# Eight query blocks moved into four Strassen pairs, with the scan beside the first output blocks and the attention beside the last

## The chip, the cores and the metric

The kernel runs on one core of one Trainium2 chip. The metric is the device time of one execution in microseconds, lower is better. TensorE (PE in the profile) multiplies matrices into PSUM; VectorE (DVE), ScalarE (ACT) and GpSimd (POOL) work on tiles in SBUF and PSUM; SyncE (SP) issues most of the DMA transfers. Each engine takes its instructions strictly in the order in which they were built.

## The reference

One layer of a hybrid decoder for 1024 prompt tokens and 8 sample tokens, which share the weights. All values are float32.

```python
def mixer_block(xn, ...):                      # xn = rmsnorm(x), width 1024
    sc_b, sc_c, sc_x, z, xbc, dt_raw, q, gates = split(xn @ w_in)
    y_a = (sc_b * conv3(sc_c * sc_x)) @ w_sc_out
    xs, bm, cm = split(silu(conv4(xbc) + bias))
    y_ssd = chunked_scan(xs, softplus(dt_raw + ...), -exp(a_log), bm, cm)   # 32 heads, 4 groups, chunks of 128
    y_b = group_rmsnorm((y_ssd + d * xs) * silu(z), groups=4) @ w_ssm_out   # 2048 -> 1024
    y_c = softmax(q @ k.T / 16) @ v  @ w_attn_o                             # 4 heads, 256 memory tokens
    g_a, g_b, g_c = split(sigmoid(gates))
    return (g_a * y_a + g_b * y_b + g_c * y_c) @ w_merge_o
x = x + mixer_block(rmsnorm(x)); x = x + swiglu(rmsnorm(x)); y = rmsnorm(x)
```

The sample tokens use their own recurrent states and their own cached keys and values (8 batches of 256 tokens).

## The kernel before

Activations lie transposed: 8 tiles of 128 features by 1032 tokens. A product in float32 precision is made of three matmuls, high times high, high times low and low times high, where a tile is split into a high part (ACT, lines 175 and 185) and a low part (DVE, lines 176 and 186).

**Two ways to make a block.** `gemm3` (lines 231 to 257) makes one block of 128 output features: 8 k-tiles, 3 thirds of 344 tokens, 3 matmuls each, so 72 matmuls of 344 columns (line 254). `strassen` (from line 379) makes two blocks at once with seven half-size products: 7 products, 4 k-tiles, 3 matmuls, two pieces of 256 and 260 tokens, so 168 matmuls (line 306). Its seven right-hand sides are called forms; one of them, T3, lies in the place of a quarter of the normalized input.

**Stages.** First the input is normalized. Then w_in is gone through in Strassen pairs: z, gates, the scan's inputs (X), the short convolution (C, B), with `gate_pair(22)` last. Then come 32 blocks of `gemm3` in a row: eight query blocks (`ps_q`, weights `wq0` to `wq7`), then three times eight output blocks, `wo00` to `wo07` (short convolution, from `sc_d`), `wo10` to `wo17` (first half of w_ssm_out, from `yb_d[0:8]`) and `wo20` to `wo27` (second half, from `yb_d[8:16]`). After them the attention output (`wo30` on, from `at_d`), the merge and the feed-forward part.

**What runs beside the 32 blocks.** A list `pend` holds small pieces, and each block takes `pace` of them at fixed places between its matmuls (`tick`). First `pend` holds the scan: four groups of eight chunks. A chunk brings small matmuls (`bp`, `xp`, `po`, `py`, `pss`), DVE and ACT work. After a group come `z_pieces` (times silu(z), sum of squares), then `group_norm`: matmuls `psny`, a root on ACT, the scaling of four tiles on DVE (line 1267) and their stores to `yb_d` (line 1270). Then `pend` holds the attention: scores `psa`, softmax, `psp`, values `psv`, and for the sample tokens keys and values read from the caches (`kc`, `vc`), scores on DVE (line 1676), `pso`, and at the end `s_back` (`psob`, line 1743), which writes the sample columns of `at_d`.

**Order.** The pieces give each instruction its place in the source order, and a scheduler with pools of buffers then sets the order on each engine. `out_in` and `out_ahead` load and split the eight inputs of a set of output blocks; the first block of a set (m = 0) goes through its k-tiles one at a time, so that it can begin when the first input is there.

Before the query blocks the T3 form must be turned back into the plain input: `again` reads four tiles again and `plain` splits them, inside `gate_pair(22)`.

Of the kernel before, what the change touches and what calls it, by code (L numbers as in the profile page):

```python
# [11 lines left out]
AF = mybir.ActivationFunctionType  # L12
# [5 lines left out]
P = 128  # L18
# [25 lines left out]
def tile_kernel(ctx: ExitStack, tc, a, o):  # L44
# [333 lines left out]

    def strassen(src1, src2, forms, nm, sums, outs, early=None, after_t3=None, ready=None, hook=None, add=False, begun=None, mid=None, t3_done=None):

# [90 lines left out]
    zs_d = dram("zs_d", [16, P, TT])  # L471
    r_d = dram("r_d", [1, TT])
    x2_d = dram("x2_d", [KD, P, TT])
# [30 lines left out]
    with tc.tile_pool(name="p0", bufs=1) as p0, tc.tile_pool(name="pop", bufs=1, space=PSUM) as pop:  # L504
# [214 lines left out]

        SY.dma_start(r_d, rbc[0:1, :])  # L720
    pmm[0] = mm_stack.enter_context(tc.tile_pool(name="pmm", bufs=2, space=PSUM))
# [182 lines left out]

    def q_step(i):
        def s():
            t = ev_tile(f"q{i}")
            gemm3(
                weights(wblock(w_in, C_Q + i * P), f"wq{i}"), xn, f"ps_q{i}",
                lambda n, c, ps: S.activation(t[:, c], ps, AF.Copy, scale=QS), *(() if i < 7 else ((0, 0, 0),)),  # L910
            )
            G.tensor_copy(qs[:, i, :], t[:, T:TT])
            S.dma_start(q_d[i], t[:, :TT])

        return [Step(wblock(w_in, C_Q + i * P), f"wq{i}", s)]

    def xbc_conv(ct, u, name):
# [31 lines left out]

    def plain_pair(col, dst, i, nm, func, hook=None, after_t3=None):  # L950

        os = []

        def outs():
            os.extend([pa_["u"](f"{nm}{i}"), pa_["u"](f"{nm}{i + 1}")])
            return os[0][:, HS[0]], os[0][:, HS[1]], None, os[1][:, HS[1]]

        pa = strassen(
            wblock(w_in, col + i * P), wblock(w_in, col + (i + 1) * P), xforms, f"{nm}{i}", pa_["s"], outs,
            hook=hook, after_t3=after_t3,  # L960
        )
        S.activation(os[0][:, :TT], os[0][:, :TT], func)
        S.dma_start(dst[i], os[0][:, :TT])
        S.activation(os[1][:, HS[1]], os[1][:, HS[1]], func)
        ins = S.activation(os[1][:, HS[0]], pa, func, scale=-1.0).ins
        S.dma_start(dst[i + 1], os[1][:, :TT])
        return ins
# [3 lines left out]

    def gate_pair(i, after_t3=None):
        return plain_pair(C_G, gt_d, i, "G", AF.Sigmoid, None, after_t3)

# [79 lines left out]
    def ssd_pieces(g, xg, bcg, hold):  # L1054
# [126 lines left out]

        out = [head] + ([None] * 4 if g == 0 else [])
        for c in range(NCK + 1):
# [146 lines left out]

    def again(rb):
        ts = []
        for kt in range(4):
            if kt % 2 == 0:
                ts.append(ev_tile(f"again{kt}"))
            b12 = ts[-1][:, HS[kt % 2]]
            SY.dma_start(b12, xT_d[kt][:, HS[1]])
            V.scalar_tensor_tensor(b12, b12, par("mix", kt), rb[:, HS[1]], op0=ALU.mult, op1=ALU.mult)
        return ts


    mem_stack = ExitStack()
# [135 lines left out]
    def load_group(g):  # L1478
        xg, bcg, _ = groups[g]
        for i, part in ((16, "ah"), (20, "al")):  # L1480
            t = act_tile(part, f"bc{i}{g}", F32)
            SY.dma_start(t, xs_d[i + g])
            bcg.append(t)
        for i in range(4):
            t = act_tile(("ah", "al")[i % 2], f"x{g}{i}", F32)

            for c in (slice(0, 2 * P), slice(2 * P, TT)) if g else (slice(0, TT),):
                SY.dma_start(t[:, c], xs_d[g * 4 + i][:, c])
            xg.append(t)

    def plain():
        loaded["wq0"] = load_raw(wblock(w_in, C_Q), "wq0")
        load_group(0)
        for kt in range(4):
# [10 lines left out]
    for name in ("ssr", "ssd", "ssy"):  # L1505
        pool[name] = ssd.enter_context(tc.tile_pool(name=name, bufs=2, side="right"))
    fillers = deque()
    for i in range(8):
        fillers.extend(q_step(i))

    acts = []

    ahead = deque()

    def out_load(src, k):
        t = ev_tile(f"in0{k}")
        SY.dma_start(t[:, :TT], src[k])
        ahead.append(t)

# [56 lines left out]

    split = []
    outs = deque()
# [16 lines left out]
    for g in range(GROUPS):  # L1595
# [888 lines left out]
```

## Time and profile before

| | |
|---|---|
| median of 3 runs | 2417.18 us (2413.96 to 2420.94) |
| the profiled execution | 2418.97 us, its span 2417.2 us |
| PE busy | 2388.3 us (99% of the span) |
| DVE busy, ACT busy | 1650.5 us (68%), 1101.1 us (46%) |
| DMA | 403.74 MB, mean 167 GB/s |
| first query block to first attention-output block (`wq0` to `wo30`) | 981.1 us to 1548.6 us of the span |

The table says that PE is nearly always busy; the profile's chain of work that ended last is 89% PE. A busy PE is not a PE at its peak, so the start times of neighbouring matmuls tell more than the busy share.

### The profile page before, as it was taken

What the parts mean: (1) busy time and instruction counts of PE and PEld (TensorE: products, weight loads), DVE (VectorE), ACT (ScalarE), POOL (GpSimd) and SP (SyncE); (2) the same over time, 40 slices, a digit from 0 to 9 for tenths busy, and PEclk for the clock granted to TensorE, in tenths of its full rate; (3) what the DMA queues carried; (4) which work ended last, traced back from release to release, by engine and by line L of the source; (5) the groups of instructions that cost most, each with busy time, mean ns of one, the idle gap of its engine ahead of it and who ended that gap; (6) DMA issues with size and microseconds to landing.
All of it is one profiled execution on the core that took longest, in us unless ns stands there. A gap on an engine that the chain in (4) does not pass through costs nothing.

```text
span 2417.2 us, 45099 instructions
## 1 busy us (share of the span) xinstructions
PE 2388.3 (99%) x18620; PEld 2305.3 (95%) x18620; DVE 1650.5 (68%) x2700; ACT 1101.1 (46%) x1794; POOL 129.3 (5%) x163
## 2 busy tenths in 40 slices
PE   8999999999999999999999999999999999999998
PEld 6999999999999999998998998899999999999998
DVE  6844677777777676568788664469687655567965
ACT  6643454555453543656656443214553333343423
POOL 0000000000000000223212000000000000000000
PEclk9999999999999999999999999999999999999999
DMA  6445423444354345768787787864346333354622
GB/s 201 140 149 166 132 88 115 134 147 128 109 158 119 101 140 167 234 214 279 257 286 238 234 321 242 276 215 145 118 159 175 103 96 105 93 182 151 194 90 78
DMA packets 348244, 403.74 MB, mean 167 GB/s; under 512 B 16014, under 2 KB 269054, under 8 KB 348031
## 3 DMA queue, kind: packets, MB, share of 16 engines
q1 hardware_dynamic: 324902, 337.60, 45.1%
q10 hardware_dynamic: 23137, 63.26, 6.8%
q8 instruction: 146, 2.39, 0.4%
q14 instruction: 59, 0.48, 0.1%
HBM read 284.65 MB, written 116.38 MB: 166 GB/s over the span
## 4 chain that ended last, share of the span: by engine, by line
PE 89%; DMA 4%; DVE 4%; ACT 1%; issue 1%; SPq 0%; ACTq 0%; DVEq 0%
PE po L254 8%; PE po L226 3%; PE ps_q L254 3%; PE pd L2295 1%; PE py L1130 1%; PE po L1121 1%; PE ps_z L226 1%; PE pss L1143 1%; PE G16m L306 1%; PE d00m L306 1%; PE G22m L306 1%; PE Z2m L306 1%; PE Z14m L306 1%; PE X4m L306 1%; PE Z12m L306 1%
## 5 line engine op out<-in xcount | busy, mean ns | idle before, releaser
L1073 ACT ACTIVATE r<-r,acum 128x128 f32<-128x128 f32 x256 | 79.3, 392 | 3.0 <-DMA r<-ac_d 2.4
L1106 POOL TENSOR_TENSOR xdd<-xdt,decst 128x512 f32<-128x512 f32 x32 | 51.1, 1596 | 248.3 <-DVE xdt L1102 246.1
L860 DVE SCALAR_TENSOR_TENSOR ax<-u,prm,ax 128x1024 f32<-128x1024 f32 x44 | 56.3, 1280 | 0.0
L1014 ACT ACTIVATE st<-st,es 128x128 f32<-128x128 f32 x128 | 41.4, 392 | 21.9 <-DMA st<-in_state_ssm_dram 19.1
L1564 DVE TENSOR_TENSOR yr<-po,yr 128x344 f32<-128x344 f32 x24 | 12.1, 514 | 45.9 <-PE po L254 32.5
L1100 DVE TENSOR_TENSOR r<-r,cbm 128x1024 f32<-128x1024 f32 x32 | 39.0, 1218 | 3.2 <-ACT r L1075 2.4
L1016 DVE SCALAR_TENSOR_TENSOR st<-sr,dts,st 128x128 f32<-128x128 f32 x128 | 40.3, 346 | 0.4
L1125 DVE TENSOR_TENSOR y<-po,ea 128x512 f32<-128x512 f32 x28 | 19.3, 689 | 25.4 <-PE po L1121 25.3
L1020 DVE SCALAR_TENSOR_TENSOR sr<-st,sr 128x128 f32<-128x128 f32 x128 | 35.3, 286 | 1.1
L1130 PE MATMUL py<-r,xdt 128*64 128x128 f32 x512 | 35.0, 279 | 0.7 <-DVE xdt L1102 0.7
L1676 DVE SCALAR_TENSOR_TENSOR kc<-kc,qb 128x256 f32<-128x256 f32 x64 | 24.2, 420 | 16.6 <-DMA qb<-qs_d 11.0
L1156 POOL TENSOR_TENSOR s<-s,cdec 128x512 f32<-128x512 f32 x28 | 34.8, 1244 | 4.1 <-DVE s L1149 3.5
L1143 PE MATMUL pss<-xdd,bT 128*128 128x512 f32 x64 | 33.0, 597 | 1.1 <-DVE y L1125 0.6
L1075 ACT ACTIVATE r<-r 128x1024 f32<-128x1024 f32 x32 | 33.8, 1056 | 0.6
L1130 PEld LDWEIGHTS py<-r,xdt 128*64 128x64 f32 x512 | 27.3, 136 | 5.0 <-DVE xdt L1102 1.4
L1121 PE MATMUL po<-bc,s 128*128 128x128 f32 x224 | 30.2, 278 | 0.8 <-DVE s L1149 0.8
L1121 PEld LDWEIGHTS po<-bc,s 128*128 128x128 f32 x224 | 28.0, 191 | 2.4 <-DVE s L1149 1.7
L1688 ACT ACTIVATE pr<-psa,mx 128x256 f32<-128x256 f32 x32 | 14.9, 473 | 29.7 <-DVE mx L1686 29.7
L863 DVE SCALAR_TENSOR_TENSOR ax<-u,prm,ax 128x1032 f32<-128x1032 f32 x22 | 28.3, 1287 | 0.0
L857 ACT ACTIVATE ax<-u,prm 128x1024 f32<-128x1024 f32 x22 | 27.4, 1246 | 1.2 <-ACT u L941 0.4
L1791 ACT CAST pTh<-psp 128x256 fp32r<-128x256 f32 x32 | 11.8, 374 | 32.9 <-DVE pTl L1792 24.0
L1102 DVE TENSOR_TENSOR xdt<-xp,dtT 128x512 f32<-128x512 f32 x32 | 22.0, 687 | 6.4 <-PE xp L1095 5.8
(8856 smaller groups left out, 9294.4 us busy)
## 6 DMA issues: line engine op xcount, KB each, us to landing
r<-ac_d SPq DMA_DIRECT2D x32, 512.0 KB
gt_d<-G ACTq DMA_DIRECT2D x24, 516.0 KB
gt<-gt_d SPq DMA_DIRECT2D x24, 516.0 KB
xs_d<-ax ACTq DMA_DIRECT2D x22, 516.0 KB
zs<-zs_d SPq DMA_DIRECT2D x16, 516.0 KB
yb_d<-x SPq DMA_DIRECT2D x16, 516.0 KB
in<-yb_d SPq DMA_DIRECT2D x16, 516.0 KB
st<-in_state_ssm_dram SPq DMA_DIRECT2D x32, 256.0 KB
```

What stands on the lines that cost most here:

```text
L226: PE.matmul(po, wt[:, ks], xc, start=(k == 0 and i == 0), stop=(k == nk - 1 and i == 2))
L254: PE.matmul(pss[t][:, :CW], wt[:, ks], x[:, c], start=(k == 0 and i == 0), stop=(k == nk - 1 and i == 2))
L306: last_mm[0] = PE.matmul(po, wt[:, ks], xc, start=(start and kt == 0 and i == 0), stop=(kt == 3 and i == 2), skip_group_check=True,).ins
L860: V.scalar_tensor_tensor(acc[:, :T], u[:, j : j + T], w[j], acc[:, :T], op0=ALU.mult, op1=ALU.add)
L1014: S.activation(st[:, i], st[:, i], AF.Copy, scale=es[:, g * 4 + i, b : b + 1])
L1016: V.scalar_tensor_tensor(st[:, i], rb, dts[:, g * 4 + i, b : b + 1], st[:, i], op0=ALU.mult, op1=ALU.add)
L1073: S.activation(r[:, j, :], r[:, j, :], AF.Relu, scale=-1.0, bias=acum[:, c, h : h + 1])
L1100: V.tensor_tensor(r, r, bc(cbm.unsqueeze(1), [P, HPG, P]), op=ALU.mult)
L1106: G.tensor_tensor(b3(xdd, HPG), b3(xdt, HPG), bc(decst[:, c, hs].unsqueeze(2), [P, HPG, 64]), op=ALU.mult)
L1121: last = PE.matmul(po[:, t * P : (t + 1) * P], state["s"][:, t * P : (t + 1) * P], bcg[1][:, cs], start=True, stop=True,)
L1130: PE.matmul(py[hp : hp + 64, (h // 2) * P : (h // 2 + 1) * P], xdt[:, h * 64 : (h + 1) * 64], r[:, (h % 2) * 4 + h // 2, :], start=True, s ...
L1143: PE.matmul(pss, bT, xdd, start=True, stop=True)
```

## The change

The eight query blocks become four pairs, `q_pair(0)`, `(2)`, `(4)`, `(6)`, through the same `strassen` as the gates, right behind `gate_pair(22)`. `again`, `plain`, `r_d` and `q_step` go. What the queries' last block had done ahead for `wo00` (loading and splitting `sc_d`) and what `plain` had done for the scan (loading group 0) now hangs on hooks inside `q_pair(6)`. The scan's pieces are spread over 14.5 output blocks (KD + 6.5) instead of 8 query blocks and 10 output blocks; the attention's pieces get what blocks are left, by the unchanged rule. The query rows of the sample tokens (`q_rows`) become a piece of the scan's beginning.

```diff
-    def strassen(src1, src2, forms, nm, sums, outs, early=None, ..., mid=None, t3_done=None):
+    def strassen(src1, src2, forms, nm, sums, outs, early=None, ..., mid=None, t3_done=None, late=None):
...
         prod(pb, wT, 512, "B22", False)
         V.tensor_tensor(o12, o12, hv(pb), op=ALU.subtract)
         tick()
+        if late is not None:
+            late()
         wD = st_split(raw2[:, 512:], f"{nm}D", 512)
         prod(pa, wD, 0, "T4", False)
...
-    def q_step(i):
-        def s():
-            t = ev_tile(f"q{i}")
-            gemm3(
-                weights(wblock(w_in, C_Q + i * P), f"wq{i}"), xn, f"ps_q{i}",
-                lambda n, c, ps: S.activation(t[:, c], ps, AF.Copy, scale=QS), *(() if i < 7 else ((0, 0, 0),)),
-            )
-            G.tensor_copy(qs[:, i, :], t[:, T:TT])
-            S.dma_start(q_d[i], t[:, :TT])
...
-    def plain_pair(col, dst, i, nm, func, hook=None, after_t3=None):
+    def plain_pair(col, dst, i, nm, func, hook=None, scale=1.0, **more):
...
-        S.activation(os[0][:, :TT], os[0][:, :TT], func)
+        S.activation(os[0][:, :TT], os[0][:, :TT], func, scale=scale)
+        if dst is q_d:
+            G.tensor_copy(qs[:, i, :], os[0][:, T:TT])
...
+    def q_pair(i, **more):
+        plain_pair(C_Q, q_d, i, "Q", AF.Copy, scale=QS, **more)
...
-        out = [head] + ([None] * 4 if g == 0 else [])
+        out = [head] + ([lambda: load_group(0, False, (2, 3)), None, q_rows, None] if g == 0 else [])
...
-    rb = ev_tile("rb")
-    SY.dma_start(rb[:, :TT], r_d.to_broadcast([P, TT]))
-    b12s = []
-    pend.append(lambda: b12s.extend(again(rb)))
+    last_gate = gate_pair(22)
+    for i in (0, 2, 4):
+        q_pair(i)
...
-    def plain():
-        loaded["wq0"] = load_raw(wblock(w_in, C_Q), "wq0")
-        load_group(0)
-        for kt in range(4):
-            split_to(*xforms["T3"][kt], b12s[kt // 2][:, HS[kt % 2]])
+    def sc_split(n):
+        for _ in range(n):
+            k = len(split)
+            split.append(split_act(ahead.popleft()[:, :TT], f"b0{k}"))
+            out_load(sc_d, k + 2)
+
+    def q_hook():
+        loaded["wo00"] = load_raw(wblock(a["w_sc_out"][0], 0), "wo00")
+        load_group(0, True, ())
+        for k in range(2):
+            out_load(sc_d, k)
 
-    last_gate = gate_pair(22, plain)
+    q_pair(6, hook=q_hook, mid=lambda: load_group(0, False, (0, 1)), late=lambda: sc_split(4))
...
-    pace[:] = len(pend) / (len(fillers) + KD + 2) + 1e-6, 0.0
-    while fillers or pend:
-        if len(fillers) == 1:
-            out_ahead(sc_d)
-        run_next(fillers, outs)
-    assert not fillers
-    q_rows()
-    flush()
+    pace[:] = len(pend) / (KD + 6.5) + 1e-6, 0.0
+    while pend:
+        run_next(outs)
```

**Where the order changes, first place: group 1's norm.** Blocks `wo10` to `wo17` need all eight tiles of `yb_d[0:8]`; tiles 4 to 7 (`b04` to `b07` once split) are group 1 of the scan. Before, on PE, group 1's `psny` stand inside block `wo01`:

```order
L254 MATMUL po_1_13026<-b00h,wo01h 128x344
L254 MATMUL po_1_13026<-b00l,wo01h 128x344
L254 MATMUL po_1_13026<-b00h,wo01l 128x344
L1244 MATMUL psny_12976<-sqa_12916,ones 128x344
L1244 MATMUL psny_12979<-sqa_12916,ones 128x344
L1244 MATMUL psny_12988<-sqa_12916,ones 128x344
L254 MATMUL po_1_13026<-b01h,wo01h 128x344
```

Now, on PE, they stand six matmuls inside `wo10` itself:

```order
L254 MATMUL po_2_13925<-b00h,wo10h 128x344
L254 MATMUL po_2_13925<-b00l,wo10h 128x344
L254 MATMUL po_2_13925<-b00h,wo10l 128x344
L1239 MATMUL psny_13684<-sqa_13616,ones 128x344
L1239 MATMUL psny_13687<-sqa_13616,ones 128x344
L1239 MATMUL psny_13696<-sqa_13616,ones 128x344
L1086 MATMUL bp_0_13799<-ident,bc_13737 128x128
L1087 MATMUL bp_0_13799<-bc_13739,bc_13737 128x128
L1090 MATMUL xp_0_13802<-ident,x_13741 128x128
L254 MATMUL po_0_14197<-b00h,wo11h 128x344
L254 MATMUL po_0_14197<-b00l,wo11h 128x344
```

The norm moved from nine blocks ahead of its reader into it. Behind these rows PE has, up to the first matmul on `b04`, 54 of line 254's matmuls (30 of `wo10` and 24 of `wo11`, which is begun early) and the small matmuls of three chunks of group 2. On SP, where the four stores of group 1 and the loads of the same tiles had stood some 60 rows apart, they now follow each other:

```order
L1265 DMA yb_d<-x_12940 128x1032
L1265 DMA yb_d<-x_12943 128x1032
L1265 DMA yb_d<-x_12946 128x1032
L1265 DMA yb_d<-x_12949 128x1032
L1478 DMA in_13794<-yb_d 128x1032
L1478 DMA in_13828<-yb_d 128x1032
L1478 DMA in_13863<-yb_d 128x1032
L1478 DMA in_13902<-yb_d 128x1032
L1062 DMA r_4_13990<-ac_d 128x1024
```

The scan's own load `r` of a later chunk stands behind them.

**Second place: group 3's norm and the first scores.** Before, on PE, group 3's `psny` end block `wo11`; `wo12` and 12 matmuls of `wo13` stand between them and the first scores `psa`:

```order
L254 MATMUL po_2_14692<-b07h,wo11l 128x344
L1244 MATMUL psny_14753<-sqa_14695,ones 128x344
L1244 MATMUL psny_14756<-sqa_14695,ones 128x344
L1244 MATMUL psny_14769<-sqa_14695,ones 128x344
L1279 MATMUL psqr_14817<-ident,qs 8x128 x4
L1279 MATMUL psqr_14823<-ident,qs 8x128 x4
L1655 MATMUL pskT_14854<-ident,kk_14785 128x128 x4
L254 MATMUL po_0_14851<-b00h,wo12h 128x344
```

Now they stand inside `wo17`, with 41 of its matmuls and 16 `pskT` behind them, and then these rows on PE, the scores beside the first matmuls of `wo20`:

```order
L254 MATMUL po_2_15417<-b07h,wo17l 128x344
L1751 MATMUL psa_0_15547<-kTh,q00h 128x256
L1752 MATMUL psa_0_15547<-kTl,q00h 128x256
L1751 MATMUL psa_1_15587<-kTh,q00h 128x256
L1752 MATMUL psa_1_15587<-kTl,q00h 128x256
L1751 MATMUL psa_2_15655<-kTh,q00h 128x256
L1752 MATMUL psa_2_15655<-kTl,q00h 128x256
L254 MATMUL po_0_15652<-b00h,wo20h 128x344
L254 MATMUL po_1_15653<-b00h,wo20h 128x344
L1753 MATMUL psa_0_15547<-kTh,q00l 128x256
```

There is no block left between the norm and what follows it, and `wo20` itself reads group 3's four tiles of `yb_d` from its fifth k-tile on.

**Third place: the end of the sample attention.** Before, on PE, `psob` stands four matmuls inside `wo27`, with 68 behind it up to `wo30`:

```order
L254 MATMUL po_0_17093<-b00l,wo27h 128x344
L254 MATMUL po_0_17093<-b00h,wo27l 128x344
L254 MATMUL po_1_17094<-b00h,wo27h 128x344
L1743 MATMUL psob<-ident,osr 128x8 x8
L254 MATMUL po_1_17094<-b00l,wo27h 128x344
```

Now 53 matmuls of `wo27` stand ahead of it on PE and 19 behind it:

```order
L254 MATMUL po_2_17225<-b05h,wo27h 128x344
L254 MATMUL po_2_17225<-b05l,wo27h 128x344
L1724 MATMUL psob<-ident,osr 128x8 x8
L254 MATMUL po_2_17225<-b05h,wo27l 128x344
L254 MATMUL po_0_17223<-b06h,wo27h 128x344
```

`psob` moved 49 matmuls towards `wo30`, whose inputs are all loads of `at_d` that follow `psob`'s own store.

More of the change, by code (lines that the diff above doesn't have):

```diff
@@ L377, in st_begin, with strassen @@
         return raw1, raw2, sa, wA, wS
-    def strassen(src1, src2, forms, nm, sums, outs, early=None, after_t3=None, ready=None, hook=None, add=False, begun=None, mid=None, t3_done=None):
+    def strassen(src1, src2, forms, nm, sums, outs, early=None, after_t3=None, ready=None, hook=None, add=False, begun=None, mid=None, t3_done=None, late=None):
         if begun is not None:
@@ L959, in plain_pair @@
             wblock(w_in, col + i * P), wblock(w_in, col + (i + 1) * P), xforms, f"{nm}{i}", pa_["s"], outs,
[L960 removed]
+            hook=hook, **more,
         )
[L962 removed]
+        S.activation(os[0][:, :TT], os[0][:, :TT], func, scale=scale)
+        if dst is q_d:
+            G.tensor_copy(qs[:, i, :], os[0][:, T:TT])
         S.dma_start(dst[i], os[0][:, :TT])
[L964 to L965 removed]
+        S.activation(os[1][:, HS[1]], os[1][:, HS[1]], func, scale=scale)
+        if dst is q_d:
+            G.tensor_copy(qs[:, i + 1, :], os[1][:, T:TT])
+        ins = S.activation(os[1][:, HS[0]], pa, func, scale=-scale).ins
         S.dma_start(dst[i + 1], os[1][:, :TT])
@@ L1471, in tile_kernel, with load_group @@
     assert not steps
-    rb = ev_tile("rb")
-    SY.dma_start(rb[:, :TT], r_d.to_broadcast([P, TT]))
-    b12s = []
-    pend.append(lambda: b12s.extend(again(rb)))
+    last_gate = gate_pair(22)
+    for i in (0, 2, 4):
+        q_pair(i)
     groups = [([], [], {}) for _ in range(GROUPS)]
-    def load_group(g):
+    def load_group(g, bcs_=True, xs_=range(4)):
         xg, bcg, _ = groups[g]
-        for i, part in ((16, "ah"), (20, "al")):
+        for i, part in ((16, "ah"), (20, "al")) if bcs_ else ():
             t = act_tile(part, f"bc{i}{g}", F32)
@@ L1483, in load_group @@
             bcg.append(t)
-        for i in range(4):
+        for i in xs_:
             t = act_tile(("ah", "al")[i % 2], f"x{g}{i}", F32)
@@ L1489, in load_group, with out_load @@
             xg.append(t)
-    def plain():
-        loaded["wq0"] = load_raw(wblock(w_in, C_Q), "wq0")
-        load_group(0)
-        for kt in range(4):
-            split_to(*xforms["T3"][kt], b12s[kt // 2][:, HS[kt % 2]])
-    last_gate = gate_pair(22, plain)
+    ahead = deque()
+    def out_load(src, k):
+        t = ev_tile(f"in0{k}")
+        SY.dma_start(t[:, :TT], src[k])
+        ahead.append(t)
+    split = []
+    def sc_split(n):
[9 more added lines that the diff above has]
+    q_pair(6, hook=q_hook, mid=lambda: load_group(0, False, (0, 1)), late=lambda: sc_split(4))
     st_stack.close()
```

24 lines of the change are left out of this document (2 added, 22 removed).

## The prediction

> **What bounds the kernel now.** I read the profile's page first, then the busy time by stretches, then the start times of neighbouring matmuls, and last the waits and the timeline at the places that the change touches. The page:
>
> ```profile
> PE 2388.3 (99%) x18620; PEld 2305.3 (95%) x18620; DVE 1650.5 (68%) x2700; ACT 1101.1 (46%) x1794; POOL 129.3 (5%) x163
> PE 89%; DMA 4%; DVE 4%; ACT 1%; issue 1%; SPq 0%; ACTq 0%; DVEq 0%
> ```
>
> The path that sets the end is the row of matmuls, so a matmul removed is time removed, and any wait of PE is time added. Now the stretch that the change rearranges (us, then busy time of PE, PEld, DVE, ACT, POOL, the granted clock, the DMA share, GB/s):
>
> ```profile
> 981.00:1064.00 83.00, 82.87 (x592) 75.75 (x593) 50.63 (x64) 48.17 (x108) 26.30 (x19) 1.00 0.68 208
> 1064.00:1149.00 85.00, 83.02 (x591) 74.59 (x590) 66.44 (x78) 54.38 (x114) 25.45 (x19) 1.00 0.80 271
> 1226.00:1316.00 90.00, 88.92 (x629) 80.41 (x628) 79.33 (x100) 54.37 (x104) 23.04 (x15) 1.00 0.78 256
> 1316.00:1420.00 104.00, 98.96 (x639) 95.60 (x638) 63.72 (x172) 49.41 (x101) 0.00 (x0) 1.00 0.79 264
> 1420.00:1548.00 128.00, 127.75 (x882) 117.49 (x881) 58.22 (x128) 37.26 (x88) 0.00 (x0) 0.99 0.77 260
> ```
>
> The query blocks (first row) leave DVE and DMA slack; the output blocks with the scan already fill DVE to 88% (79.33 of 90), and the attention fills DMA to 0.79. The change takes the roomy blocks out of this row and leaves scan and attention with 24 blocks instead of 32. PE waited for others in two places worth naming:
>
> ```profile
> PE po L254 <- ACT yr L1562: 3.1, 1, 3.1
> PE psa L1770 <- ACT q01h L185: 1.4, 1, 1.4
> ```
>
> Parts 2 to 6 below are waits of an engine that works strictly in order through a fixed number of matmuls: none of them can fall below nothing.
>
> **Part 1, the matmuls saved.** The pace of each form comes from rows without waits: a stretch of Strassen pairs, and matmuls of line 254 in `wo17` and `wo20`.
>
> ```profile
> 840.00:880.00 40.00, 40.00 (x339) 40.00 (x337) 1.00 0.52 159
> 1410.83 0.32 PE L254 MATMUL po<-b05h,wo17l 128*128 128x344 f32 x1
> 1416.00 0.32 PE L254 MATMUL po<-b01h,wo20l 128*128 128x344 f32 x1
> 1419.39 0.66 PE L254 MATMUL po<-b00h,wo20h 128*128 128x344 f32 x1 [3.07 <-ACT yr L1562]
> 1419.85 0.49 PE L254 MATMUL po<-b00l,wo20h 128*128 128x344 f32 x1
> 1422.43 0.46 PE L254 MATMUL po<-b01l,wo20h 128*128 128x344 f32 x1
> 1420.00:1425.00 5.00, 5.00 (x29) 5.00 (x28) 3.90 (x5) 3.96 (x6) 0.00 (x0) 0.73 0.82 258
> ```
>
> 40.00 us over 337 weight loads is 0.1187 us a Strassen matmul; from 1410.83 to 1416.00 are 33 steps, 0.1567 us each. Two query blocks cost 144 x 0.1567 = 22.56 us, a pair 168 x 0.1187 = 19.94 us: 2.62 us less, and four pairs give **-10.5 us**, all of it on the path. The scan's and the attention's own matmuls stay. `again` and `plain` ran on DVE, ACT and SP under PE's matmuls, so their going gives nothing by itself.
>
> [...]
>
> The same rows show what an idle PE costs here: after 3.07 us of idling, nine steps from 1419.85 to 1422.43 took 0.287 us each, and the granted clock was 0.73 in that stretch. The whole episode is 3.2 us of waiting and 12 matmuls at 0.13 us extra, 1.6 us. This wait is of `wo20` on an eviction queued on ACT; that place is reordered, so I drop it: **-4.8 us**. Each longer new wait is charged 1.6 us for the clock.
>
> **Part 2, the hand-over from the last pair to `wo00`.** Before, the hand-over to the first query block cost 0.4 us:
>
> ```profile
> L254 PE MATMUL ps_q<-xnh,wq0h 128*128 128x344 f32 x24 | 8.0, 332 | 0.4 <-ACT G L965 0.4
> ```
>
> The hooks split eight inputs at 1.23 us each on DVE (the row of `q00l` in part 4) while PE runs the last two products, 48 x 0.1187 = 5.7 us, and then 9 x 0.157 = 1.4 us for each input. Splitting keeps up if the loads do; behind it the scan's first chunk now starts with nothing else to do. From 0 to 5 us (half of the splits behind the products); I take **+2 us**.
>
> **Part 3, group 1's norm inside `wo10`.** Before, the chain behind group 2's `psny`, which began just ahead of the first row, ran like this on DVE (start, duration, count):
>
> ```profile
> 1231.44 1.49 DVE L1245 TENSOR_SCALAR y<-psny 128x344 f32<-128x344 f32 x3
> 1237.54 1.23 DVE L126 TENSOR_TENSOR sqa<-y,sqa 128x1032 f32<-128x1032 f32 x1 [3.66 <-ACT sqa L125]
> 1240.45 4.90 DVE L1267 SCALAR_TENSOR_TENSOR x<-x,prm,sqa 128x1032 f32<-128x1032 f32 x4
> 1172.90:1205.40 32.50, 32.50 (x262) 1.00 0.74 225
> ```
>
> From T0, about 1230.6, to the first scaled tile 11 us, to the last 15 us. For store, load back and split the nearest rows are those of `psob` in part 5, 11.7 us less `psob` itself and a copy, 10.5 us. So `b04` is there between T0 + 11 + 10.5 = 21.5 and, since SP issues all four stores ahead of the loads, T0 + 15 + 10.5 = 25.5; I take 24, and 26 if DVE, which in the new order has two more splits and three chunks' work ahead, comes late. PE's cover: 54 x 0.157 = 8.5 us, `psny` 1.6 us, and some 92 records of scan matmuls at (32.50 - 72 x 0.157) / 190 = 0.11 us, 10.3 us (last row: one block with its scan pieces). That makes 20.4, so PE idles 3.6 to 5.6 us and loses 1.6 us of clock. `psny` itself waits for eleven DVE operations of 1.23 us plus a split and three evictions, 16 us, behind 77 matmuls of 0.157 us, so up to 3 us more. Bounds 2 to 13 (in order, PE cannot gain by it); I take **+8 us**.
>
> [...]
>
> **Part 4, group 3's norm ahead of `wo20`.** The same chain with the same neighbours as now, before:
>
> ```profile
> 1313.29 1.90 PE L1244 MATMUL psny<-sqa,ones 128*128 128x344 f32 x6
> 1325.28 4.90 DVE L1267 SCALAR_TENSOR_TENSOR x<-x,prm,sqa 128x1032 f32<-128x1032 f32 x4
> 1330.09 1.23 DVE L186 TENSOR_TENSOR q00l<-qT,q00h 128x1032 fp32r<-128x1032 f32 x1
> L1676 DVE SCALAR_TENSOR_TENSOR kc<-kc,qb 128x256 f32<-128x256 f32 x64 | 24.2, 420 | 16.6 <-DMA qb<-qs_d 11.0
> ```
>
> From T0 = 1313.3 the four tiles are scaled at +16.9 and the first query tile's low part is there at +18. The new order has the same sequence on DVE, and then the splits of `wo20`'s first inputs, to +20. PE's cover was a block and 12 matmuls; now it is `psny` 1.6, 41 x 0.157 = 6.4 and 16 `pskT`, 1.8 us: 9.8. So PE waits about 8 to 10 us. Then 42 scores, a probability transpose and 33 matmuls of `wo20` (10.7 us) stand ahead of `b04`, to +30.5. Its low part stands on DVE, from +18 on, behind six splits of 1.23 us, five sample scores of 0.42 us and softmax steps, near +29 to +31, and `b05` to `b07` follow more slowly than PE's 1.4 us each: another 0 to 4 us. Clock 1.6, and the 1.4 us wait of before goes. Bounds 4 to 16; I take **+11 us**.
>
> **Part 5, `psob` close to `wo30`.**
>
> ```profile
> 1536.95 0.66 PE L1743 MATMUL psob<-ident,osr 8*128 8x8 f32 x8
> 1548.64 0.94 PE L254 MATMUL po<-b00h,wo30h 128*128 128x344 f32 x3
> ```
>
> Copy, store to `at_d`, load and split took no more than 11.7 us, and 68 matmuls (10.7 us) covered it. Now 19 matmuls cover 3.0 us and the 8 of `psob` 0.6: 8 us open, 1.6 us of clock. Bounds 2 (if `psob` comes early) to 11; I take **+9 us**.
>
> **Part 6, a denser attention.** Its transfers from 1316 to 1560 us (count and size of each):
>
> ```profile
> vc<-in_cache_mem_v_dram SPq DMA_DIRECT2D x16, 512.0 KB
> kc<-in_cache_mem_k_dram SPq DMA_DIRECT2D x14, 512.0 KB
> qT<-q_d SPq DMA_DIRECT2D x8, 516.0 KB
> qb<-qs_d SPq DMA_DIRECT2D x8, 512.0 KB
> at_d<-ot ACTq DMA_DIRECT2D x8, 512.0 KB
> ```
>
> DMA worked 0.79 x 104 + 0.77 x 128 = 181 us in the 232 us from `wo12` to `wo27`. Six blocks leave with 12 transfers of about 0.52 MB, at 264 / 0.79 = 334 GB/s 19 us, so 162 us remain. The matmuls left take 8.5 x 11.3 + (232 - 14 x 11.3) = 170 us, and with the waits of parts 4 and 5 about 190. So DMA would be at 0.85 to 0.95, and what hides it is those very waits. Behind a late cache tile stand DVE's scores, then all softmax work, then PE. From 0 to 12 us; I take **+2 us**.
>
> **Sum.** -10.5 - 4.8 + 2 + 8 + 11 + 9 + 2 = +16.7 on the profiled execution's 2418.97 us (its span 2417.2 and 1.8 around it), 2435.7. That execution lies 1.8 us above the median of the runs, so I forecast 2433.9, say **2434 us**.
>
> **The rivals.** *A, the waits are covered (faster).* For it: the scheduler began `wo11` ahead of `wo10`'s second half and put scores ahead of `wo20`, so some idling is filled, and the second stretch above shows PE unhurt beside a DMA share of 0.80. Then -10.5 - 4.8 + 2 = -13, 2404 us; it decides if parts 3 to 5 together stay under 6 us. Against it: the chains of 24, 18 and 11.7 us are read from this trace, and covers of 20, 10 and 4 us from the order. *B, the waits only eat the gain (no change).* Each chain runs shorter than here, about 14 us in all: 2418 us. *C, DMA sets the attention's pace (slower still).* Its 162 us run at no better than 0.80 of the time, as in the busiest stretch above: 200 us instead of 190, then 2444, and with the bounds of parts 3 to 5 up to 2455; it decides when the cache loads reach PE through `pso` or `psa`. For it: the 54 transfers above fell on 14 blocks and now fall on 8.5. Against: the idle PE of parts 4 and 5 gives DMA its time.
>
> **How the numbers follow.** About 0.3%, 7.3 us, is what a measurement tells from no change: faster is under 2410, slower over 2424.4. Forecast (2425 to 2444) 0.54, A 0.16, B 0.14, C 0.16. Faster 0.16, same 0.14, slower 0.70. For 8 in 10 the range takes in B, most of C, and leaves out two thirds of A: 2408 to 2452.
>
> **What would show it.** Right: four pairs named Q at 0.119 us a matmul; PE idle over 3 us ahead of `b04` in `wo10`, ahead of the first `psa` or `wo20`, and ahead of `wo30`, each followed by 3 us at half the granted clock; PE busy share under 99%. Wrong: no such gaps (A), or gaps before `pso` and `psa` released by DMA through all of `wo20` to `wo26` (C), or Strassen pairs that themselves wait.

## The result

The changed kernel takes 2456.1 us (median), the kernel before 2417.2 us: a ratio of 1.016 (95% interval 1.0142 to 1.0177), 38.8 us slower. The forecast was 2434 us with 2408 to 2452, so the direction was right and the size too small, outside the range. The profiled execution took 2455.84 us (span 2454.1) against 2418.97 us, 36.9 us more, where the prediction's sum said 16.7. One execution of the first experiment below took 2597 us at a granted clock of 0.85, in a slower state of the chip, and is left out of that experiment's median.

The page of the changed kernel, the engines' busy time and the chain that ended last:

```profile
PE 2390.1 (97%) x18716; PEld 2300.8 (94%) x18716; DVE 1670.5 (68%) x2728; ACT 1111.5 (45%) x1798; POOL 121.3 (5%) x163
PE 84%; DVE 7%; DMA 6%; ACT 2%; issue 1%; SPq 0%; ACTq 0%; DVEq 0%
```

PE fell from 99% to 97% of a longer span, and PE's share of the chain from 89% to 84%; DVE and DMA took it. The list of PE's waits between 960 and 1590 us shows what for (total, times, longest):

```profile
PE xp L1090 <- DMA x<-xs_d: 8.1, 6, 3.0
PE po L254 <- ACT b00h L185: 7.7, 2, 6.8
PE psp L1765 <- DVE pr L1675: 7.0, 5, 3.4
PE pskT L1636 <- DMA kk<-k_d: 4.9, 1, 4.9
PE po L254 <- DVE b03l L186: 3.7, 1, 3.7
PE po L254 <- DVE b00l L186: 2.2, 1, 2.2
PE psa L1751 <- ACT q00h L185: 1.8, 1, 1.8
PE po L254 <- DVE b01l L186: 1.2, 1, 1.2
PE pso L1707 <- DMA vc<-in_cache_mem_v_dram: 1.2, 3, 0.7
PE po L1116 <- DVE s L1144: 1.0, 1, 1.0
PE psp L1765 <- ACT pTh L1772: 1.0, 1, 1.0
```

These are 39.8 us; in the kernel before the whole list had two waits above 0.8 us there, 3.1 and 1.4. By stages (us, then busy time of PE, PEld, DVE, ACT, POOL, the granted clock, the DMA share, GB/s):

```profile
980.50:1059.50 79.00, 79.00 (x665) 79.00 (x664) 35.50 (x42) 35.38 (x51) 2.21 (x8) 1.00 0.52 174
1220.10:1284.00 63.90, 54.46 (x375) 45.16 (x374) 52.72 (x68) 45.05 (x100) 19.84 (x13) 0.95 0.76 257
1394.00:1430.00 36.00, 27.48 (x159) 25.37 (x158) 30.70 (x56) 22.46 (x43) 0.00 (x0) 0.86 0.87 309
1430.00:1560.00 130.00, 120.41 (x814) 105.52 (x813) 76.12 (x229) 44.91 (x115) 0.00 (x0) 1.00 0.84 278
```

The four pairs run without a gap at 0.1188 us a matmul, as forecast. The loss lies behind them: around `wo10` (second row), at the seam of `wo17` and `wo20` (third) and in the attention (fourth). Waits also cost clock. Four stretches of the same view:

```profile
1224.30:1227.70 3.40, 3.40 (x6) 2.02 (x7) 1.95 (x5) 1.40 (x2) 0.00 (x0) 0.50 1.05 405
1244.70:1248.10 3.40, 3.40 (x15) 3.40 (x14) 1.40 (x3) 0.00 (x0) 1.04 (x1) 0.51 1.03 403
1326.70:1330.10 3.40, 3.17 (x12) 3.11 (x13) 0.00 (x0) 0.00 (x0) 0.00 (x0) 0.50 1.02 395
1398.00:1412.00 14.00, 9.67 (x40) 8.61 (x41) 12.54 (x13) 6.17 (x8) 0.00 (x0) 0.63 0.75 265
```

The first three are 3.4 us at half the granted clock each, behind idle PE of 2.2 and 0.5, 3.7 and 3.0 us. In the third, matmuls of line 254 start 0.288 us apart (1327.49 to 1329.79) instead of 0.157; so, as an estimate, such a stretch costs half its length at full work, 1.7 us. The fourth, at the seam, holds some 10 us of it, in part while PE waited. The kernel before had one such stretch between 960 and 1550 us, the one behind its wait at `wo20` (0.54 from 1419.60 to 1423.00).

### The profile page after: what moved, and what is told of

Read it like the earlier page. It is cut to its first block, busy times and chain, and to the rows that moved or that the text cites. A ratio compares the mean times of both kernels' runs of the same rounds, so it can differ in the third digit from the quotient of the medians.

```text
span 2454.1 us, 45305 instructions
## 1 busy us (share of the span) xinstructions
PE 2390.1 (97%) x18716; PEld 2300.8 (94%) x18716; DVE 1670.5 (68%) x2728; ACT 1111.5 (45%) x1798; POOL 121.3 (5%) x163
## 4 chain that ended last, share of the span: by engine, by line
PE 84%; DVE 7%; DMA 6%; ACT 2%; issue 1%; SPq 0%; ACTq 0%; DVEq 0%
PE po L254 6%; PE po L226 3%; PE py L1125 1%; PE pd L2276 1%; DMA qb<-qs_d 1%; PE po L1116 1%; PE ps_z L226 1%; DMA x<-xs_d 1%; PE G16m L306 1%; PE pss L1138 1%; DVE kc L1657 1%; PE d00m L306 1%; PE Z2m L306 1%; PE Z14m L306 1%; PE X18m L306 1%
## 5 line engine op out<-in xcount | busy, mean ns | idle before, releaser
L1120 DVE TENSOR_TENSOR y<-po,ea 128x512 f32<-128x512 f32 x28 | 19.3, 689 | 24.1 <-PE po L1116 22.8
L1094 ACT COPY bT<-bp 128x128 f32<-128x128 f32 x32 | 8.3, 261 | 55.1 <-DVE cbm L1092 54.9
L1090 PE MATMUL xp<-ident,x 128*128 128x128 f32 x128 | 21.7, 278 | 8.1 <-DMA x<-xs_d 8.1
```

## The experiments

Three theories stood at the start. *Theory 1*: the pairs give their 10.5 us, and the spread of scan and attention over 24 blocks instead of 32 takes more than that, in a few waits with a place each. *Theory 2*: the loss sits in the pairs or in the hand-over from them to `wo00`. *Theory 3*: every block that scan and attention lose costs a fixed price. Ratios are against runs of the kernel before beside each run; differences to the changed kernel are against its 2456.1 us.

### The spread without the pairs

```diff
-    pace[:] = len(pend) / (len(fillers) + KD + 2) + 1e-6, 0.0
-    while fillers or pend:
+    pace[:] = 0, 0.0
+    while fillers:
...
+    pace[:] = len(pend) / (KD + 6.5) + 1e-6, 0.0
+    while pend:
+        run_next(outs)
```

> Undoes the Strassen half alone: the eight query blocks are plain blocks again, but nothing runs beside them, and the scan and the attention are spread over the 24 output blocks as in the changed kernel. Theory 1 (the pairs give their 10.5 us and the spread over 24 blocks takes all of the loss): 2456 + 10.5 = 2466 us (2462 to 2471), with the same waits in wo10, wo14, wo17, wo20 and wo30. Theory 2 (the loss sits in the pairs or in the hand-over from them to wo00): most of the loss goes, 2430 us or less.

Measured 2463.3 us, ratio 1.0191 (1.0172 to 1.0210). Theory 1 holds, theory 2 falls: the spread alone costs 47 us, and the pairs take 7.2 us of it back. The largest waits of PE carry the names of the changed kernel's: 6.6 us for `b00h`, 5.3 before `psp`, 4.5 before `pskT`. The stretch of the eight bare blocks, beside the pairs' 79.00 us above:

```profile
979.50:1070.30 90.80, 90.80 (x577) 90.80 (x578) 17.07 (x15) 26.43 (x38) 6.25 (x7) 1.00 0.52 169
```

The pairs with their hand-over (`Q0` at 979.3, `wo00` at 1059.4 us) are 10.7 us shorter, the predicted gain; `wo00` itself then takes 20.6 us instead of 17.0 and gives some of it back.

### Fewer pairs

One, two or three pairs, the other query blocks plain with the scan beside them (two pairs shown; one pair: KD + 2, three: KD + 5):

```diff
+    for i in range(0, 2, 2):
+        q_pair(i)
...
+    q_pair(2, plain)
...
-    for i in range(8):
+    for i in range(4, 8):
...
-    pace[:] = len(pend) / (len(fillers) + KD + 2) + 1e-6, 0.0
+    pace[:] = len(pend) / (len(fillers) + KD + 4) + 1e-6, 0.0
```

> Only the first four query blocks become two pairs; the other four stay plain blocks with the scan beside them, the scan is spread over these four and 12 output blocks, the attention over the last 12. Group 1's norm then stands four blocks ahead of wo10, group 3's four ahead of wo20. Theory 1 (what costs is a norm or a load next to its reader): the gain of two pairs, 5.2 us, is kept and few waits are left: 2413 us (2408 to 2420). Theory 3 (each block that scan and attention lose costs its share, because DVE or DMA sets their pace): half of the 49 us that eight blocks cost, less 5.2: 2417 - 5 + 25 = 2437 us.

> Six query blocks as three pairs, the last two as plain blocks beside the scan, which is spread over these two and 13 output blocks. In the order of PE the four norms (psny) then stand in wo02, wo06, wo12 and wo16; with two pairs they stood in wo00, wo04, wo10 and wo14, with four in wo04, wo10, wo13 and wo17. Theory 4 (a norm costs where it falls into the first block of a set, wo00, wo10 or wo20): nothing is lost in wo00 and wo10, so three pairs come out below two: 2417 - 8 + 20 (attention, wo30, hand-over) = 2430 us. Theory 3 (a price of 6.1 us for each block that scan and attention lose): 2417 - 8 + 37 = 2446 us, halfway between two pairs (2437) and four (2456).

> Two query blocks as one pair, six as plain blocks; the scan over these six and ten output blocks (16 instead of 18 before), the attention over 14 as before. The norms stand in wq6, wo02, wo06 and wo12, none in the first block of a set. Theory 4: the gain of one pair, 2.6 us, is kept nearly whole: 2415 us (2412 to 2418), a little faster than the kernel before. Theory 3: two blocks at 6.1 us less 2.6: 2426 us.

| pairs | time (us) | ratio (interval) | against before, without the pairs' 2.62 us each | per block lost |
|---|---|---|---|---|
| 1 | 2421.9 | 1.0020 (1.0011 to 1.0029) | +7.7 | 3.9 |
| 2 | 2436.8 | 1.0081 (1.0063 to 1.0098) | +25.2 | 6.3 |
| 3 | 2445.5 | 1.0121 (1.0108 to 1.0134) | +36.6 | 6.1 |
| 4 | 2456.1 | 1.0160 (1.0142 to 1.0177) | +49.8 | 6.2 |

(The fourth column is the time less 2416.8 us, plus 2.62 us a pair; the last column divides it by all blocks lost so far.) Theory 1 forecast 2413 us for two pairs and missed by 24. I then formed *theory 4*, that a group's norm costs where it meets the first block of a set; it forecast three pairs below two, and missed; one pair came out between theory 4's 2415 us and theory 3's 2426. Theory 3's average price came out in size each time except for the first pair. Pair by pair the column grows by 7.7, 17.5, 11.4 and 13.2 us, so it is not one price for every block: the first pair takes both its blocks from the scan, the second both from the attention, the third one from each, the fourth half a block from the scan and one and a half from the attention. And theory 3 names no mechanism: with three pairs PE waits 9.0 us for the evictions `yr` behind ACT, with four for the things listed above. The next runs ask what the waits are.

### wo10: the chain or DVE's queue

```diff
-    ins = (..., (yb_d, a["w_ssm_out"][0, 0:D]), ...)
+    ins = (..., (sc_d, a["w_ssm_out"][0, 0:D]), ...)
```

> The changed kernel, but wo10 to wo17 read the short convolution's tiles instead of the first half of the normed scan output, so that their loads wait for no store of group 1 (its stores and everything else stay; the output is another). The prediction's step (the chain norm, store, load back, split holds wo10): the 9 us of idle PE in wo10 and some 3.4 us of half clock go, 2444 us. The rival (the splits of the first four inputs stand behind the scan's steps on DVE, whatever they read): the waits before b00l, b01l and b03l stay and the time is within 3 us of 2456.

Measured 2458.0 us, ratio 1.0170. The waits of PE from 1215 to 1265 us are those of the changed kernel:

```profile
PE po L254 <- DVE b03l L186: 3.7, 1, 3.7
PE po L254 <- DVE b00l L186: 2.2, 1, 2.2
PE po L254 <- DVE b01l L186: 1.3, 1, 1.3
```

The prediction's chain falls, the rival holds. What stands ahead of these splits on DVE shows in the changed kernel's timeline (start, duration; the row on ACT makes the high part of the tile `b03`):

```profile
1219.05 1.23 DVE L1227 TENSOR_TENSOR sqa<-sqa,zs 128x1032 f32<-128x1032 f32 x1
1220.20 1.23 DVE L1219 TENSOR_TENSOR x<-x,zs 128x1032 f32<-128x1032 f32 x1
1221.34 1.23 DVE L186 TENSOR_TENSOR b00l<-in,b00h 128x1032 fp32r<-128x1032 f32 x1
...
1231.54 1.23 DVE L186 TENSOR_TENSOR b02l<-in,b02h 128x1032 fp32r<-128x1032 f32 x1
...
1235.56 1.04 ACT L185 CAST b03h<-in 128x1032 fp32r<-128x1032 f32 x1
...
1237.45 5.68 DVE L1262 SCALAR_TENSOR_TENSOR x<-x,prm,sqa 128x1032 f32<-128x1032 f32 x4
1243.05 1.22 DVE L186 TENSOR_TENSOR b03l<-in,b03h 128x1032 fp32r<-128x1032 f32 x1
```

`b00l` stands behind the gating, `b03l` behind the four scalings of group 1, work that none of these tiles needs: the high part of `b03` was there at 1236.60 us (1235.56 + 1.04), and `b03l` starts at 1243.05, as the last of the four scalings ends (1237.45 + 5.68 = 1243.13). The positive test:

```diff
-        pend.append(lambda g=g, hold=hold: [z_load(g, t, hold) for t in range(2)])
+        pend.append(lambda g=g, hold=hold: [z_load(g, t, hold) for t in range(2) if g != 1])
...
+        if g == 1:
+            pend.extend([None] * 8 + [lambda xg=xg: [SY.dma_start(yb_d[4 + t], xg[t]) for t in range(4)]])
+            continue
```

> The changed kernel without the gating and the norm of group 1: its four tiles are stored as they are (left out: 23 us of DVE work and PE's three psny; the stores, the loads and the splits of wo10 stay). Theory 4 (the splits of wo10's first inputs stand behind this work on DVE): the 9.4 us of idle PE in wo10 and two windows of half clock of 1.7 us go, 2456 - 13 = 2443 us. The rival (the loads of the yb_d tiles land late because SP and DMA are busy): the waits stay, 2455 us.

Measured 2437.3 us, 18.8 less, and in the same window no wait of `wo10` is left:

```profile
PE po L1116 <- DVE s L1141: 0.8, 1, 0.8
PE xp L1090 <- DMA x<-xs_d: 0.7, 1, 0.7
```

The 18.8 us are more than these waits and their clock, some 11 us. The run leaves out more than DVE's part: seven operations of ACT go, 7.5 us in the changed kernel (1213.29 to 1233.90 us), the four loads of group 1's `zs` go, and the wait of `pskT` falls from 4.9 to 2.3 us. So 18.8 us is not the price of the waits in `wo10` alone. That DVE's order makes them rests on this run, the unchanged waits of the run before it, and the rows of `b03` together.

### The attention: the query row, the memory tiles, the end

```diff
+            if b:
+                qbs[b] = qbs[0]
+                SY.dma_start(qx_d[b], qs_d[b : b + 1, :].to_broadcast([P, D]))
+                return
             qbs[b] = at.tile([P, D], F32, tag="qb", bufs=1, name=f"qb{b}")
```

> The changed kernel with the sample scores of all eight tokens made with the first token's query row; the seven other broadcast rows are still moved, 512 KB each, but to a place that nobody waits for (left out: the right queries). Theory 5 (the one buffer of the query row: its load starts when the scores of the token before are done and lands 6.5 us later, DVE waits for it with the softmax steps behind it, and PE's psp behind those): the 7 us of idle before psp go, 2456 - 7 = 2449 us. Rival C of the prediction (DMA's throughput sets the attention's pace): the bytes are the same, within 2 us of 2456.

Measured 2447.2 us, ratio 1.0125, 8.9 less. The stretch of the fourth stage above, in this run:

```profile
1430.00:1560.00 130.00, 128.00 (x879) 114.63 (x879) 79.59 (x238) 48.63 (x125) 0.00 (x0) 1.00 0.81 274
```

PE works 128.0 of 130 us instead of 120.4, at nearly the same DMA share (0.81 and 0.84), so throughput did not set this pace. In the changed kernel the one buffer can be seen on SP, DVE and PE (the load's issue, the score that waits for it, the softmax step behind it, PE):

```profile
1477.52 0.33 SPq L1646 DMA_DIRECT2D qb<-qs_d  x1
1484.18 0.42 DVE L1657 SCALAR_TENSOR_TENSOR kc<-kc,qb 128x256 f32<-128x256 f32 x1 [3.15 <-DMA qb<-qs_d]
1488.22 0.60 DVE L1675 TENSOR_SCALAR pr<-pr,mx 128x256 f32<-128x256 f32 x2
1488.70 0.72 PE L1765 MATMUL psp<-ident,pr 128*128 128x128 f32 x4 [3.38 <-DVE pr L1675]
```

The list of PE's waits names DVE; two steps further back it is a transfer. The memory tiles:

```diff
     def kv_ahead(m):
+        if m:
+            kv_load[m] = kv_load[0]
+            return
```

> The changed kernel with the memory's second half of keys and values replaced by the first (left out: two loads of 512 KB, and the second half of the memory). Theory 6 (the 4.9 us before the second pskT are the late load of kk, whose buffer comes free late; ACT waits for its neighbour vv with group 3's root behind it, so the norm comes late too): these 4.9 us, most of the 2.7 us before psa and wo20 and two windows of half clock go, 2456 - 9 = 2447 us. The prediction's part 4 (group 3's norm on DVE ends last): the idle comes back in front of psa, q00l and wo20, within 2 us of 2456.

Measured 2452.4 us, ratio 1.0153 (1.0136 to 1.0169), 3.7 less: between the two, and not clear of the scatter (2450.0 to 2456.8 us; the profiled execution is the longest). In its profile the wait of `pskT` is gone, and most of it stands again in front of the first scores and `wo20` (1385 to 1430 us):

```profile
PE po L254 <- DVE b00l L186: 3.9, 1, 3.9
PE psa L1754 <- ACT q00h L185: 2.9, 1, 2.9
```

So by this trace two chains end there almost together: the late `kk`, and the prediction's norm of group 3. Why `kk` is late is read on SP: `vv` waits 6.5 us for a buffer whose store to `yr_d` has not landed, and `kk` stands behind it.

```profile
SPq L1578 <- DMA yr_d<-yr: 6.5, 1, 6.5
1392.46 0.33 SPq L1578 DMA_DIRECT2D vv<-v_d  x1
1393.36 0.53 SPq L1579 DMA_DIRECT2D kk<-k_d  x1
1399.30 1.94 PE L1636 MATMUL pskT<-ident,kk 128*128 128x128 f32 x8 [4.92 <-DMA kk<-k_d]
```

The end of the attention:

```diff
-        pace[:] = len(pend) / (len(outs) - 1.4) + 1e-6, 0.0
+        pace[:] = len(pend) / (len(outs) - 2.2) + 1e-6, 0.0
```

> The changed kernel with the attention's pieces spread over 0.8 of a block less, so that psob stands 63 matmuls ahead of wo30 instead of 19. If the wait at wo30 is the chain psob, copy, store, load, split (11.7 us against 3 us of cover): 6.8 us of idle and 3.4 us of half clock go, the attention gets some 10% denser and loses about 2: 2448 us (2445 to 2451). If DMA sets the attention's pace, the wait comes back ahead of pso and psp: within 2 us of 2456.

Measured 2446.2 us, ratio 1.0122 (1.0102 to 1.0142), 9.8 less: the chain of `psob` is the cause of the wait at `wo30`. Of the row of the changed kernel

```profile
1585.54 1.23 PE L254 MATMUL po<-b00h,wo30h 128*128 128x344 f32 x3 [6.80 <-ACT b00h L185]
```

only waits of 0.8 us and less are left there. Not all of the 9.8 us is this wait: the waits of `psp` for `pr` fell from 7.0 to 3.7 us as well.

### Moving blocks between scan and attention

```diff
-    pace[:] = len(pend) / (KD + 6.5) + 1e-6, 0.0
+    pace[:] = len(pend) / (KD + 4.5) + 1e-6, 0.0
```

> The changed kernel with the scan spread over 12.5 output blocks instead of 14.5, the attention over 11.5 instead of 9.5 (less 1.4 by the unchanged rule). Group 1's norm then stands 62 matmuls ahead of wo10 instead of inside it, group 3's some 250 ahead of wo20 instead of 60. Theory 4 (what costs is a group's norm on DVE falling together with the eight splits of a set's first block, and the loads of the attention's beginning falling together with the last norm): in wo10 6 us less idle, ahead of wo20 6 us, the attention's psp 5 us, wo30 6 us, half clock 7 us less, the denser scan costs 8 us: 2456 - 30 + 8 = 2434 us. Theory 3 (each block that one of the two loses costs the same 6 us, whichever it is): the scan loses what the attention gains, within 5 us of 2456.

Measured 2451.1 us, ratio 1.0143, 5.0 less: just theory 3's bound, not theory 4's 2434. That it gained at all says that a block is worth more to the attention than to the scan. The attention's waits shrank (`psp` to 2.5 us, `pskT` off the list), and the scan got new ones:

```profile
PE po L254 <- ACT yr L1549: 9.5, 3, 6.4
PE xp L1090 <- DMA x<-xs_d: 6.5, 5, 2.3
PE po L254 <- DVE gt L1547: 4.1, 1, 4.1
PE po L1116 <- DVE s L1141: 4.1, 2, 3.4
```

### All four at once, and a control

> A control: the kernel before with the three left-out parts of the runs on the norm, the query rows and the memory (group 1's gating and norm, seven of the eight query rows with their bytes kept, the memory's second half with its loads). If these parts lie beside PE's matmuls in the kernel before, it gains only the three psny, about 1.5 us, and perhaps a micro-second of short waits: 2414 us (2410 to 2417). If they gain much here too, what they gained in the changed kernel was not a wait of the new order.

> The changed kernel with all four at once: the same three parts left out, and the attention ending 0.8 of a block earlier. If the waits stand one behind the other and each was priced by its own run (10, 18, 9 and 4 us): 2456 - 41 = 2415 us (2410 to 2422), level with the kernel before, and what is left of the loss are the hand-over and the late x tiles, about the 10.5 us that the pairs give. If a wait that goes uncovers the next one: 2428 us or more.

The control took 2410.3 us (ratio 0.9977, 0.9968 to 0.9987), 6.5 us less than before, at the edge of what was expected: some of the left-out work was on the path there too. The changed kernel with all four took 2421.3 us (1.0019, 1.0010 to 1.0028), 34.8 less, where the four runs alone add to 41; they overlap by 6 us. Against the control (which needs no earlier end, since `psob` has its cover there) it is 11 us slower, of 38.8. So about 28 us of the loss belong to these four places; the pairs' gain included, some 21 us of waits are elsewhere, 7.0 us of them before `xp` in this run.

### Giving the cover back

Four blocks beside the scan, four beside the attention, or all eight are computed twice and the first product is dropped, with the pace slowed to match:

```diff
+        if nm in ("02", "05", "12", "15"):
+            gemm3(w_, acts, f"pc{nm}", lambda n, c, ps: None)
         gemm3(w_, acts, f"po{nm}", part,
...
-    pace[:] = len(pend) / (KD + 6.5) + 1e-6, 0.0
+    pace[:] = len(pend) / (KD + 6.5 + 4) + 1e-6, 0.0
```

> The changed kernel with four blocks of PE work added beside the scan: wo02, wo05, wo12 and wo15 are computed twice, the first product is thrown away, and the scan's pieces are spread over 18.5 blocks instead of 14.5. 288 matmuls at 0.157 us are 45.1 us more on PE. If each block of cover takes 6 us of waits away, also here: 2456 + 45 - 24 = 2477 us. If the loss lies on the attention's side (DMA at 0.9 there): 2456 + 45 - 5 = 2496 us. If it lies on the scan's side: 2456 + 45 - 35 = 2466 us.

> The same with wo21, wo23, wo25 and wo26 computed twice, and the attention's pieces spread over four blocks more; the scan as in the changed kernel. 6 us a block on either side: 2477 us. The loss on the attention's side: 2466 us. On the scan's side: 2496 us.

> Both: eight blocks computed twice, 90.2 us more on PE, so that scan and attention have 32 blocks again, as in the kernel before, and the four pairs stay. If cover is all that the pairs took away: the kernel before plus 90.2 less the pairs' 10.5, 2417 + 90 - 10 = 2497 us (2494 to 2503). If something else in the changed order costs (hand-over, late x tiles), 2456 + 90 - 30 = 2516 us or more.

| cover added | time (us) | against 2456.1 | added PE work | taken off the waits |
|---|---|---|---|---|
| four beside the scan | 2488.7 | +32.6 | 45.1 | 12.5 (3.1 a block) |
| four beside the attention | 2481.9 | +25.8 | 45.1 | 19.3 (4.8 a block) |
| both | 2519.4 | +63.3 | 90.2 | 26.9 |

Both sides pay, the attention more, as the pairs one by one showed, and none of the three expected cases for one side was met. Cover is not all: of the 49 us (38.8 and the pairs' 10.5) only 27 come back, and 2519 us is 22 more than the kernel before with this work added and the pairs' gain taken off. What waits there in spite of 32 blocks:

```profile
PE pskT L1638 <- DMA kk<-k_d: 6.5, 1, 6.5
PE po L254 <- DVE b03l L186: 4.7, 1, 4.7
PE xp L1090 <- DMA x<-xs_d: 4.3, 5, 1.9
PE psa L1753 <- ACT q00h L185: 1.6, 1, 1.6
```

These have a fixed place in the new order, whatever the density: the end of the scan against the loads of `wo20`, a norm against the first block of a set, the hand-over to `wo00`. That they are the 22 us is read from this list, not tested.

### The wait that the prediction dropped

```diff
-            acts.append(split_act(ahead.popleft()[:, :TT], f"b0{k}"))
+            with tc.issue_after(evict[0]) if src is ins[2][0] else nullcontext():
+                acts.append(split_act(ahead.popleft()[:, :TT], f"b0{k}"))
...
-            if k > 1:
+            if k > 1 and (src is not ins[2][0] or k < 4):
...
-                S.copy(t[:, c], ps)
+                evict[0] = S.copy(t[:, c], ps).ins
```

> The kernel before, with the splits of wo20's inputs from the third on put behind the last eviction of wo17 on ACT, so that this eviction no longer stands behind a split that waits 8.7 us for its load. If the 3.07 us of idle PE at wo20 and the half clock behind it are that queue: 2417 - 4.7 = 2412 us (2411 to 2415). If the loads of the next inputs then end last: within 1.5 us of 2417.

Measured 2417.4 us, ratio 1.0003 (0.9994 to 1.0012). The wait of 3.07 us is gone, and PE has two shorter ones; ACT, which makes the high parts, now waits for the loads themselves (1400 to 1440 us):

```profile
PE po L254 <- DVE b06l L186: 0.8, 1, 0.8
PE po L254 <- DVE b04l L186: 0.5, 1, 0.5
ACT b04h L185 <- DMA in<-yb_d: 2.8, 1, 2.8
ACT b06h L185 <- DMA in<-yb_d: 1.9, 1, 1.9
ACT b05h L185 <- DMA in<-yb_d: 1.3, 1, 1.3
```

The time is the rival's. From 1410 to 1440 us PE works 27.98 of the 30 us, at a granted clock of 1.00; in the kernel before it works 26.93, and the clock is 0.89 up to 1425 us. So part of the 4.7 us came through there, and the times of the runs do not show it; that the late loads take the rest is not shown.

No run beat the kernel before with the whole computation done.

## Why the prediction was too low

In the prediction's own terms, these steps failed. Part 6 was the term most out, a wait of the attention put at +2 us that measured 9. A wait for group 3's x tiles, 4.7 us, was put at nothing, without a reason. Part 2, put at +2, measured 5.4. Part 3, put at +8, measured 11 by another path than the one priced. Together with 0.8 us of part 5 these are the 18.9 us between the sum of 16.7 and the sum at the end of this account.

**Part 1** was right: -10.5 forecast, 10.7 us from the trace, 7.2 as the difference of two kernels with `wo00` in it. The -4.8 us for the old wait at `wo20`: that wait is not in the changed kernel's list, so the term stays in the sum below, but it was no gain to count on, for taking only that queue away in the kernel before changed nothing.

**Part 2**, +2 us: the waits of PE from 1060 to 1080 us hold one row above the rest,

```profile
PE xp L1090 <- DMA x<-xs_d: 3.7, 2, 2.0
```

and with a window of half clock (0.51 from 1074.00 to 1077.40 us) that is 5.4 us. What waited was not a split but group 0's third and fourth x tiles, whose loads the change made a piece of the scan (SP issues them from 1061.2 to 1067.0 us). In the run without the pairs, where all four are loaded at once as before, PE works 15.65 of the 17.0 us of `wo00`, at a granted clock of 1.00; here it works 16.86 of 20.6, at 0.92. I had written of the splits and of the scan's first chunk, not of those two loads.

**Part 3**, +8 us, had nearly the size (8 us of idle and two windows, about 11) by the wrong mechanism. I followed the chain to `b04`; PE stopped at `b00`, `b01` and `b03`, which depend on nothing new and stood behind group 1's work on DVE. The step that failed is "PE's cover up to `b04`": the order on DVE, not on PE alone, had to be read for the first four inputs. The sign that I had named, over 3 us of idle PE ahead of `b04`, did not appear; 3.7 us stood ahead of `b03`'s low part.

**A term that was missing**: group 3's x tiles. On SP the last four of their loads stand right behind the four stores of group 2's scaled tiles, which wait for DVE's scaling (issued from 1317.9 to 1321.9 us, the loads from 1322.0), so a norm delays PE here too, one group later, and it reached `xp`: 3.0 us and a window of half clock, 4.7.

**Part 4**, +11 us: 4.9 + 1.8 + 0.9 us of idle, and of the 9.9 us at a granted clock of 0.50, in 8.4 of which PE worked, by estimate 3 to 4 lost, 11. The size held; of the idle, the larger part carried the name of `kk`, which the prediction did not mention, with its norm chain right behind (the profile of the run on the memory tiles).

**Part 5**, +9 us: 9.8 by the run that ended the attention earlier; the trace has 6.8 us of idle and 1.9 us of half clock (0.51 from 1582.50 to 1589.50 us, with PE at work in 3.96), 8.7, and that run's waits before `psp` were shorter too.

**Part 6**, +2 us of a range from 0 to 12, is the term most out: 9 us (7.0 and 1.0 before `psp`, 1.2 before `pso`), and 8.9 by the run with one query row. Its words named the path, a late transfer, DVE's scores, softmax, PE, but I judged it by the DMA share, and the transfer was the query row's, not a cache tile's. It hangs on one buffer whose 6.7 us from issue to use lie open once less of PE's work covers them. Rival C came near the time (2444, at most 2455) by throughput, which that run excludes for this wait; that it came nearer than the forecast is luck.

Added up, the terms come to -10.5 - 4.8 + 5.4 + 11 + 4.7 + 11 + 9.8 + 9 = 35.6 of the 36.9 us measured (parts 5 and 6 overlap a little, as part 5 says). A middle or low value was taken for each unknown, and none came out clearly lower; that all of them hang on the cover and so are high together is my reading, which no run tests. The range took 2452 as its end where the upper bounds stood higher.

On the clock, each longer new wait was charged 1.6 us. Half clock came here after 3.03 us, after 1.78 and 1.96 us (1071.60 and 1073.88), and after 2.19 and 0.48 us with five matmuls between, while after 3.38 us before `psp` (1488.70) the granted clock stayed at 1.00. So in this trace the length of a wait alone does not tell whether the clock falls, and two short waits in `wo10` cost it as well.

## What to carry to other kernels

Matmuls that run beside latency-bound work are its cover. Before making them cheaper or moving them away, price each block by what it hides: here a block taken away took 11.3 us of cover with it and cost about 6 us in new waits on average, against 1.3 us that its faster form saved. And read the order of the engine that feeds PE at the place where a new set begins: an input with no new dependency also waits: the high part of `b03` was there at 1236.60 us here, and its low part started at 1243.05, behind the work put ahead of it.

## What was not expected

The average price of a lost block looked steady, 6.1 to 6.3 us from two to four pairs, although other waits appeared each time. It is an average over unlike steps, 3.9, 8.7, 5.7 and 6.6 us a block from pair to pair; why the step that took two blocks from the attention alone cost most stays open. A stretch of 3.4 us at half clock (0.50 from 1224.30) followed two waits of PE of 2.2 and 0.5 us, and none followed one of 3.4 us (1.00 from 1488.70 to 1492.20). And a load of 512 KB took 6.7 us from its issue to its reader here (1477.52 to 1484.18) while the DMA share of the surrounding stretch was 0.84.
